# From the output projection to the FFN: the last unit's sums kept apart, second PSUM banks, narrow idle products, wide closing sums, and the first decays one unit later

## The chip, the cores and the metric

The kernel runs on one core of a Trainium2 chip. The metric is the device time of one launch in microseconds (us). Five engines work side by side, each through its own queue in order: TensorE (PE, matrix products), VectorE (DVE), ScalarE (ACT), GpSimd (POOL) and SyncE (SP, which issues most transfers). Engines wait for each other through semaphores. Products land in PSUM, which has eight banks; everything else on the chip lies in SBUF.

## What is computed

One layer of a hybrid diffusion backbone, for 128 context tokens and 256 latent tokens of width 2048 (T = 384 tokens in all):

```python
mod = silu(cond) @ w_ada + b_ada                 # sh1, sc1, ga1, sh2, sc2, ga2
h = rmsnorm(x, norm_pre_mix) * (1 + sc1) + sh1
m, s_f, s_b = mixer(h, ...)                      # gated linear attention and a 2-D DFT branch,
                                                 # merged by sigmoid gates, then @ w_out
x = x + ga1 * rmsnorm(m, norm_post_mix)
h = rmsnorm(x, norm_pre_ffn) * (1 + sc2) + sh2
ff = (silu(h @ w_ffn_gate) * (h @ w_ffn_up)) @ w_ffn_down
x = x + ga2 * rmsnorm(ff, norm_post_ffn)
```

The attention needs a decay per token and channel: `log_sigmoid(lr @ w_a2 + b) / 16`, summed along the tokens of a chunk. The change touches the two lines in the middle (the second norm of the mixer's output and the norm ahead of the FFN), the attention's first decays, and the last norm.

## The kernel before, in words

All activations lie transposed: 128 channels on the partitions, the 384 tokens along the free axis, so a width of 2048 is KT = 16 tiles of 128x384. Weights come in blocks of 128x1024 (512 KB). Each float32 block is split into a high part `whi` (ACT, line 224) and a rest `wlo` (DVE, line 225), and each product is made of three passes: high by high, high by rest, rest by high (`gemm`, line 258). The order of the work on PE, ACT, DVE and POOL is written out by hand in the program; SP's transfers are issued in program order too. Side work runs as Python generators that are advanced by one turn after each half unit of products (`step`): the adaptive modulation of later stages (`ada_rest`, each turn two DVE instructions over 1024 columns, a cycle of 18 turns), and in the gate stage the attention (`gla`).

**Gate stage.** 32 gate units of two halves each advance `gla` and the modulation by a turn. Per head, `gla` makes the decay logits `z` on PE (line 649), turns them into `la` on ACT and DVE (lines 657 to 661), splits `la` into `lah` and `lal`, and in the next turn PE sums them along the tokens (`bT`, line 671), for the forward and then for the backward direction. A head takes 14 turns, and the last norm another three.

**Output projection.** 16 units `m = w_out @ merged`, each followed by `wout`: the tile's square is added to `qs[0]`, the tile times the gate `ga1` goes to `mg32(i)`, its product with `x1(i)` to `qs[1]`, and its square to `qs[2]`. The last unit is followed by `wout_last`: it leaves the square in a tile of its own, forms the other two from the bank with the gate as an operand, ACT and DVE by turns, and adds to `qs[1]`.

**Passage to the FFN.** `wide_sum` sums `qs` over the channels on PE (a product with ones, 64 columns); the results lie in the banks `pst[0]` and `pst[1]`. From the first sum follows the factor `r[:, 0]` (a root on ACT, a reciprocal on DVE); `rows2` spreads it over the partitions (`prow`). From the other two sums and the first factor follows, in four small DVE steps, the mean square of the new `x`, so `r[:, 1]` and the second spread `prow2`. `res_m` and `res_a` form the new x1 tile: DVE multiplies `mg32(k)` by `prow`, and POOL (DVE for tile 0) adds it to `x1(k)`. Then `mg32` of the last tile is made on DVE (line 1147).

**Head of the FFN.** The first three FFN units (HEAD = 3) run side by side over the 16 tiles, nine products a tile (line 1201). `res_b` normalises tile k into `z` (DVE; ACT scales and shifts, lines 1169 and 1173) and gives the high part `h2[0]`; `res_c` gives the rest `h2[1]`. Tiles 0, 9 and 12 (`fused`) take another form: DVE scales, ACT shifts, each in two pieces (128 and 256 tokens) in one bank (lines 1161 and 1165). x1 runs three tiles ahead (LAG = 3): three tiles are made before tile 0 is normalised.

**FFN and end.** The rest of the FFN follows unit by unit. At the end `tok_sum` sums the squares (one column, line 292), `r3` and its spread `prowE` follow, and the tiles of the output are finished on three routes (PE, POOL and DVE) and stored through ACT's and SP's queues.

Of the kernel before, what the change touches and what calls it, by code (L numbers as in the profile page):

```python
# [11 lines left out]
F32 = mybir.dt.float32  # L12
# [84 lines left out]
def tile_step(ctx: ExitStack, tc: tile.TileContext, a, o):  # L97
# [498 lines left out]
    with ExitStack() as s:  # L596
# [23 lines left out]
        def gla():  # L620
# [10 lines left out]
            for h in range(NH):  # L631
# [387 lines left out]
    with ExitStack() as s:  # L1019
# [28 lines left out]
        def wout_last(p, i):  # L1048

            sq0, sq2 = (pe.tile([P, T], F32, tag="sq", name="sq") for _ in range(2))  # L1050
            pr = pe.tile([P, T], F32, tag="sg", name="pr")
            ACT.activation(sq0, p, AF.Square)
# [11 lines left out]
        for i in range(KT):  # L1064
            p = psm.tile([P, T], F32, tag="mm", name="pmm")
            for g in range(2):
# [20 lines left out]
                if g:  # L1087
                    if i < KT - 1:
                        wout(p, i)
                    else:  # L1090
                        sq0, sq2 = wout_last(p, i)
                step(ada)
            if i == KT - 4:
                for _ in ada_gen:
# [1 line left out]

        pst = [pss.tile([P, 2, 3, 64], F32, tag="side", name=f"pst{n}") for n in range(2)]

        def wide_sum(dst, src):
            for t in range(3):
                PE.matmul(dst[:, t, :], src[:, t * P : (t + 1) * P], ones[:, 0:64], start=True, stop=True)

        r = pe.tile([P, 2, 3], F32, name="r12", bufs=1)
        u = pe.tile([P, 2, 3], F32, name="u12", bufs=1)
# [9 lines left out]
        DVE.tensor_copy(u[:, 0, :], pst[0][:, 0, :, 0])  # L1116
# [4 lines left out]
        DVE.tensor_add(qs[2], qs[2], sq2)  # L1121
        wide_sum(pst[1][:, 1], qs[2])
        rows2(prow, 0)
        DVE.scalar_tensor_tensor(u[:, 0, :], pst[1][:, 1, :, 0], 0.5, r[:, 0, :], op0=ALU.mult, op1=ALU.mult)
        DVE.tensor_add(u[:, 0, :], u[:, 0, :], pst[1][:, 0, :, 0])
        DVE.scalar_tensor_tensor(u[:, 1, :], u[:, 0, :], 2.0 / D, r[:, 0, :], op0=ALU.mult, op1=ALU.mult)
        DVE.tensor_add(u[:, 1, :], u[:, 1, :], msx)

        t1s = {}

# [4 lines left out]
        def res_a(k):  # L1135

            (POOL if k else DVE).tensor_add(x1(k), t1s.pop(k), x1(k))

        res_m(0)
        rsqrt(r[:, 1, :], u[:, 1, :], 1.0)  # L1140
        rows2(prow2, 1)
        for k in range(3):
            if k:
                res_m(k)
            res_a(k)
        for lo, hi, c in segs:
            DVE.tensor_scalar_mul(mg32(KT - 1)[:, lo:hi], p[:, lo:hi], mods[:, 2, KT - 1, c : c + 1])

        h2 = alloc_A()
        hp = [  # L1150
            (pss if u == 0 else psm).tile([P, T], F32, tag="mm" if u else "side", name="pmm") for u in range(HEAD)
        ]
        zt = [pss.tile([P, T], F32, tag="side", name="z") for _ in range(2)]
        fused = (0, 9, 12)

        def res_b(k):

            z = zt[k % 2]
            if k in fused:
                for lo, hi, c in segs:  # L1160
                    DVE.scalar_tensor_tensor(
                        z[:, lo:hi], x1(k)[:, lo:hi], mods[:, 4, k, c : c + 1], prow2[:, lo:hi],
                        op0=ALU.mult, op1=ALU.mult,
                    )
                    ACT.activation(h2[0][:, k, lo:hi], z[:, lo:hi], AF.Identity, bias=mods[:, 3, k, c : c + 1])
            else:
                DVE.tensor_mul(z, x1(k), prow2)
                for lo, hi, c in segs:
                    ACT.activation(
                        z[:, lo:hi], z[:, lo:hi], AF.Identity,  # L1170
                        bias=mods[:, 3, k, c : c + 1], scale=mods[:, 4, k, c : c + 1],
                    )
                ACT.copy(h2[0][:, k, :], z)

        def res_c(k):
            z = zt[k % 2]
            if k in fused:
                for lo, hi, c in segs:
                    DVE.scalar_tensor_tensor(
                        h2[1][:, k, lo:hi], z[:, lo:hi], mods[:, 3, k, c : c + 1], h2[0][:, k, lo:hi].bitcast(F32),  # L1180
                        op0=ALU.add, op1=ALU.subtract,
# [2 lines left out]
                DVE.tensor_sub(h2[1][:, k, :], z, h2[0][:, k, :].bitcast(F32))  # L1184


        LAG = 3
# [99 lines left out]
        DVE.tensor_copy(r3, pst[:, 0:3])  # L1287
        DVE.tensor_add(r3, r3, pys[0][:, 0:3])
        rsqrt(r3, r3, 1.0 / D)
        put(pe_ks[0], psm, "mm")  # L1290
        for t in range(3):
# [117 lines left out]
```

## Time and profile before

| | us |
|---|---|
| median of 3 runs | 2034.55 (2034.52 to 2034.64) |
| the profiled execution | 2032.79 |
| its span, first to last instruction | 2031.0 |
| PE busy | 2014.6 (99%) |
| DVE busy | 1251.2 (62%) |
| ACT busy | 770.4 (38%) |
| POOL busy | 34.2 (2%) |

The page of the profile lists busy time per engine over the span. Other views answer for a stretch: the list of waits (engine, line and tile that waited, what ended the wait, total, times, longest), the timeline (start, duration, engine, line, operation, output and inputs, shape, count, and in brackets the idle time before it and what ended it), and stretches (length, busy time of PE, weight loads, DVE, ACT and POOL, then the granted clock of PE as a share of full speed, then transfers). PEld is the loading of weights into PE. A float32 product shows as two passes. Ends of PE instructions are modelled, since products overlap.

### The profile page before, as it was taken

What the parts mean: (1) busy time and instruction counts of PE and PEld (TensorE: products, weight loads), DVE (VectorE), ACT (ScalarE), POOL (GpSimd) and SP (SyncE); (2) the same over time, 40 slices, a digit from 0 to 9 for tenths busy, and PEclk for the clock granted to TensorE, in tenths of its full rate; (3) what the DMA queues carried; (4) which work ended last, traced back from release to release, by engine and by line L of the source; (5) the groups of instructions that cost most, each with busy time, mean ns of one, the idle gap of its engine ahead of it and who ended that gap; (6) DMA issues with size and microseconds to landing.
All of it is one profiled execution on the core that took longest, in us unless ns stands there. A gap on an engine that the chain in (4) does not pass through costs nothing.

```text
span 2031.0 us, 30079 instructions
## 1 busy us (share of the span) xinstructions
PE 2014.6 (99%) x12236; PEld 1959.9 (96%) x12236; DVE 1251.2 (62%) x1655; ACT 770.4 (38%) x1144; POOL 34.2 (2%) x46
## 2 busy tenths in 40 slices
PE   8999999999999999989999999999999999999999
PEld 5779999999999999989999999999999999999998
DVE  5669787898677778866444545453545454544345
ACT  4233545443346544446233222222222222222235
POOL 0000000000000000002000000000000000000001
PEclk9999999999999999999999999999999999999999
DMA  9978677767546785533444444443444444433332
GB/s 390 371 254 276 206 239 233 246 223 261 210 154 207 256 282 185 193 125 115 145 148 147 151 146 147 151 148 125 145 145 146 147 149 150 138 133 125 126 130 97
DMA packets 112395, 373.94 MB, mean 184 GB/s; under 512 B 13692, under 2 KB 32316, under 8 KB 108160
## 3 DMA queue, kind: packets, MB, share of 16 engines
q1 hardware_dynamic: 111248, 370.64, 53.2%
q8 instruction: 96, 1.57, 0.3%
q10 hardware_dynamic: 1008, 1.38, 0.2%
q14 instruction: 43, 0.35, 0.0%
HBM read 358.34 MB, written 13.63 MB: 183 GB/s over the span
## 4 chain that ended last, share of the span: by engine, by line
PE 98%; ACT 1%; DVE 1%; issue 0%; DMA 0%; ACTq 0%; DVEq 0%
PE pmm L258 67%; PE pdn L258 18%; PE pv L399 3%; PE pf L258 2%; PE pgm L382 1%; PE pmm L1201 1%; PE px L417 1%; PE px L300 0%; PE po L629 0%; PE pr L564 0%; PE py L1278 0%; PE pgm L496 0%; PE dl L629 0%; PE pp L856 0%; PE px L870 0%; PE bT L671 0%
## 5 line engine op out<-in xcount | busy, mean ns | idle before, releaser
L258 PE MATMUL pmm<-A_hi,whi 128*128 128x384 f32 x2480 | 831.8, 335 | 0.0
L258 PE MATMUL pmm<-A_hi,wlo 128*128 128x384 f32 x2480 | 828.9, 334 | 0.0
L258 PE MATMUL pmm<-A_lo,whi 128*128 128x384 f32 x2480 | 828.8, 334 | 0.0
L225 DVE TENSOR_TENSOR wlo<-raw,whi 128x1024 fp32r<-128x1024 f32 x434 | 529.8, 1223 | 416.8 <-ACT whi L224 415.6
L224 ACT CAST whi<-raw 128x1024 fp32r<-128x1024 f32 x436 | 457.5, 1050 | 582.4 <-PE pmm L258 226.9
L258 PEld LDWEIGHTS pmm<-A_hi,whi 128*128 128x128 f32 x2480 | 465.6, 188 | 2.9 <-issue 1.8
L258 PEld LDWEIGHTS pmm<-A_lo,whi 128*128 128x128 f32 x2480 | 465.7, 188 | 0.2
L258 PEld LDWEIGHTS pmm<-A_hi,wlo 128*128 128x128 f32 x2480 | 465.6, 188 | 0.0
L556 DVE SCALAR_TENSOR_TENSOR adacc<-adaw,spad,adacc 128x1024 f32<-128x1024 f32 x240 | 296.9, 1278 | 1.2 <-DMA adaw<-in_w_ada 1.0
L258 PE MATMUL pdn<-hid_hi,whi 128*128 128x384 f32 x704 | 235.2, 334 | 0.0
L258 PE MATMUL pdn<-hid_hi,wlo 128*128 128x384 f32 x704 | 235.1, 334 | 0.0
L258 PE MATMUL pdn<-hid_lo,whi 128*128 128x384 f32 x704 | 235.1, 334 | 0.0
L258 PEld LDWEIGHTS pdn<-hid_hi,whi 128*128 128x128 f32 x704 | 132.2, 188 | 0.4 <-issue 0.4
L258 PEld LDWEIGHTS pdn<-hid_lo,whi 128*128 128x128 f32 x704 | 132.2, 188 | 0.0
L258 PEld LDWEIGHTS pdn<-hid_hi,wlo 128*128 128x128 f32 x704 | 132.2, 188 | 0.0
L284 ACT CAST hid_hi<-hfE 128x384 fp32r<-128x384 f32 x44 | 22.6, 513 | 164.0 <-DVE hfE L1224 164.0
L1224 DVE TENSOR_TENSOR hfE<-sg,pmm 128x384 f32<-128x384 f32 x44 | 24.4, 555 | 84.6 <-PE pmm L258 84.0
L1216 ACT ACTIVATE sg<-pmm 128x384 f32<-128x384 f32 x44 | 21.6, 492 | 136.3 <-PE pmm L258 136.2
L1241 DVE TENSOR_TENSOR Blo<-Blo,pdn 128x384 f32<-128x384 f32 x72 | 39.5, 553 | 47.9 <-PE pdn L258 47.9
L1241 DVE TENSOR_TENSOR Bhi<-Bhi,pdn 128x384 f32<-128x384 f32 x72 | 39.1, 549 | 34.1 <-PE pdn L258 34.0
L258 PE MATMUL pmm<-o_hi,whi 128*128 128x384 f32 x128 | 42.8, 335 | 0.0
L258 PE MATMUL pmm<-o_lo,whi 128*128 128x384 f32 x128 | 42.8, 334 | 0.0
(309 smaller groups left out, 1520.9 us busy)
## 6 DMA issues: line engine op xcount, KB each, us to landing
adaw<-in_w_ada SPq DMA_DIRECT2D x128, 512.0 KB, 3.9
raw<-in_w_g SPq DMA_DIRECT2D x88, 512.0 KB, 3.2
raw<-in_w_u SPq DMA_DIRECT2D x88, 512.0 KB, 3.3
raw<-in_w_d SPq DMA_DIRECT2D x88, 512.0 KB, 3.2
slab<-in_w_ada SPq DMA_DIRECT2D x32, 1024.0 KB
raw<-in_w_gate SPq DMA_DIRECT2D x64, 512.0 KB, 4.5
raw<-in_w_in SPq DMA_DIRECT2D x44, 512.0 KB, 3.2
raw<-in_w_out SPq DMA_DIRECT2D x32, 512.0 KB, 4.5
```

Of the source, the lines that this page charges most:

```text
L224: ACT.copy(hi, raw)
L225: sub = lambda: eng.tensor_sub(lo, raw, hi.bitcast(F32))
L258: PE.matmul(dst, w[wi][:, k * n + n0 : k * n + n0 + P], x[xi][:, k0 + k, :], start=first and k == 0 and j == 0, stop=last and k == kts - 1 ...
L284: ACT.copy(hi, src)
L382: PE.matmul(pgv[q : q + 32, :], spad[:, k, :], slab[k // (KT // 2)][:, k % (KT // 2), :], start=k < 4, stop=k >= KT - 4,)
L399: PE.matmul(pv[2 * t + g], hT[x_][:, kb, t * P : (t + 1) * P], w_[:, g * 512 : (g + 1) * 512], start=kb == 0 and j == 0, stop=kb == KT - 1 ...
L417: PE.matmul(px, w_[:, u * P : (u + 1) * P], hT[x_][:, kb, :], start=j == 0, stop=j == 2)
L556: DVE.scalar_tensor_tensor(acc[:, c, :], w, spad[:, k, c : c + 1], acc[:, c, :], op0=ALU.mult, op1=ALU.add,)
L1201: PE.matmul(hp[u], hw[u][j][:, ((k - 1) % 8) * P : ((k - 1) % 8 + 1) * P], h2[m][:, k - 1, :], start=k == 1 and j == m == 0, stop=k == KT ...
L1216: ACT.activation(sgs[j], p, AF.Silu)
L1224: DVE.tensor_mul(hf, sgs.pop(j), p)
L1241: DVE.tensor_add(acc(k), acc(k), p)
```

## The change

It has five edits.

1. In the attention, head 0 gives up two turns between the decays' split and the first `bT` products; all that follows in `gla` comes two turns later.
2. `wout_last` now makes `mg32` of the last tile on ACT, as in the other units, and returns three tiles (the square, room for the product with x1, and the square of `mg32`). ACT reads the bank alone. The three sums have banks of their own (`E0`, `S0`) or share one that is read when both are there (`S12`). The addition to `qs[1]` and `qs[2]` is done ahead of one sum each, and the sum of the last square is added between them. The scaling of line 1147 is gone.
3. The banks of the head units are taken earlier, and PE makes narrow products of ones by ones (128 columns) into one of them: two after `prow`, four after `prow2`. The head's first product starts that bank anew.
4. Two x1 tiles instead of three are made before tile 0 is normalised; the third follows right behind it. The second piece of a fused tile has a bank of its own (`zx`).
5. At the end `wide_sum` (64 columns) takes the place of `tok_sum`.

```diff
                 split_act(lah, lal, la)
                 yield
+                if h == 0:
+                    yield
+                    yield
                 for d in range(2):
...
             ACT.activation(sq0, p, AF.Square)
             for lo, hi, c in segs:
-                g = mods[:, 2, i, c : c + 1]
-                DVE.scalar_tensor_tensor(pr[:, lo:hi], p[:, lo:hi], g, x1(i)[:, lo:hi], op0=ALU.mult, op1=ALU.mult)
-                ACT.activation(sq2[:, lo:hi], p[:, lo:hi], AF.Square, scale=g)
-            DVE.tensor_add(qs[1], qs[1], pr)
-            return sq0, sq2
+                ACT.mul(mg32(i)[:, lo:hi], p[:, lo:hi], mods[:, 2, i, c : c + 1])
+            ACT.activation(sq2, mg32(i), AF.Square)
+            return sq0, pr, sq2
...
-        wide_sum(pst[0][:, 0], qs[0])
-        DVE.tensor_copy(u[:, 0, :], pst[0][:, 0, :, 0])
-        wide_sum(pst[0][:, 1], sq0)
-        DVE.tensor_add(u[:, 0, :], u[:, 0, :], pst[0][:, 1, :, 0])
+        wide_sum(E0[:, 0], qs[0])
+        wide_sum(S0[:, 0], last3[0])
+        DVE.tensor_copy(u[:, 0, :], E0[:, 0, :, 0])
+        DVE.tensor_mul(last3[1], mg32(KT - 1), x1(KT - 1))
+        for n in (1, 2):
+            DVE.tensor_add(qs[n], qs[n], last3[n])
+            wide_sum(S12[:, n - 1], qs[n])
+            if n == 1:
+                DVE.tensor_add(u[:, 0, :], u[:, 0, :], S0[:, 0, :, 0])
         rsqrt(r[:, 0, :], u[:, 0, :], 1.0 / D)
-        wide_sum(pst[1][:, 0], qs[1])
-        DVE.tensor_add(qs[2], qs[2], sq2)
-        wide_sum(pst[1][:, 1], qs[2])
         rows2(prow, 0)
...
+        def narrow_warm(n):
+            for _ in range(n):
+                PE.matmul(hp[1][:, 0:P], ones, ones, start=True, stop=True)
+
+        narrow_warm(2)
         res_m(0)
-        rsqrt(r[:, 1, :], u[:, 1, :], 1.0)
+        rsqrt(r[:, 1, :], u[:, 0, :], 1.0)
         rows2(prow2, 1)
-        for k in range(3):
+        narrow_warm(4)
+        LAG = 3
+        for k in range(LAG - 1):
             if k:
                 res_m(k)
             res_a(k)
-        for lo, hi, c in segs:
-            DVE.tensor_scalar_mul(mg32(KT - 1)[:, lo:hi], p[:, lo:hi], mods[:, 2, KT - 1, c : c + 1])
...
+        zx = psm.tile([P, T], F32, tag="mm", name="zx")
+        def z_of(k, lo):
+            return zx if lo else zt[k % 2]
...
         for k in range(KT + 1):
             if k < KT:
                 res_b(k)
+            if k == 0:
+                res_m(LAG - 1)
+                res_a(LAG - 1)
             if k:
                 res_c(k - 1)
...
-        tok_sum(pst[:, 0:3], qs[0], *late)
-        tok_sum(pys[0][:, 0:3], last_sq)
+        pst, ps2 = (t.rearrange("p (t c) -> p t c", t=3)[:, :, 0:64] for t in (pst, pys[0]))
+        wide_sum(pst, qs[0], *late)
+        wide_sum(ps2, last_sq)
```

More of the change, by code (lines that the diff above doesn't have):

```diff
@@ L1090, in tile_step @@
                     else:
-                        sq0, sq2 = wout_last(p, i)
+                        last3 = wout_last(p, i)
                 step(ada)
@@ L1095, in tile_step, with wide_sum @@
                     pass
-        pst = [pss.tile([P, 2, 3, 64], F32, tag="side", name=f"pst{n}") for n in range(2)]
-        def wide_sum(dst, src):
+        E0, S0, S12 = (pss.tile([P, 2, 3, 64], F32, tag="side", name="pst") for _ in range(3))
+        def wide_sum(dst, *src):
             for t in range(3):
-                PE.matmul(dst[:, t, :], src[:, t * P : (t + 1) * P], ones[:, 0:64], start=True, stop=True)
+                for n, x in enumerate(src):
+                    PE.matmul(
+                        dst[:, t, :], x[:, t * P : (t + 1) * P], ones[:, 0:64], start=n == 0, stop=n == len(src) - 1,
+                    )
         r = pe.tile([P, 2, 3], F32, name="r12", bufs=1)
@@ L1137, in res_a @@
             (POOL if k else DVE).tensor_add(x1(k), t1s.pop(k), x1(k))
+        hp = [
+            (pss if u == 0 else psm).tile([P, T], F32, tag="mm" if u else "side", name="pmm") for u in range(HEAD)
+        ]
+        def narrow_warm(n):
+            for _ in range(n):
+                PE.matmul(hp[1][:, 0:P], ones, ones, start=True, stop=True)
+        narrow_warm(2)
         res_m(0)
-        rsqrt(r[:, 1, :], u[:, 1, :], 1.0)
+        rsqrt(r[:, 1, :], u[:, 0, :], 1.0)
         rows2(prow2, 1)
-        for k in range(3):
+        narrow_warm(4)
+        LAG = 3
+        for k in range(LAG - 1):
             if k:
@@ L1160, in res_b @@
                 for lo, hi, c in segs:
+                    z = z_of(k, lo)
                     DVE.scalar_tensor_tensor(
@@ L1178, in res_c @@
                 for lo, hi, c in segs:
+                    z = z_of(k, lo)
                     DVE.scalar_tensor_tensor(
@@ L1283, in tile_step @@
         last_sq = late.pop()
-        tok_sum(pst[:, 0:3], qs[0], *late)
-        tok_sum(pys[0][:, 0:3], last_sq)
+        pst, ps2 = (t.rearrange("p (t c) -> p t c", t=3)[:, :, 0:64] for t in (pst, pys[0]))
+        wide_sum(pst, qs[0], *late)
+        wide_sum(ps2, last_sq)
         r3 = pe.tile([P, 3], F32, name="r3", bufs=1)
-        DVE.tensor_copy(r3, pst[:, 0:3])
-        DVE.tensor_add(r3, r3, pys[0][:, 0:3])
+        DVE.tensor_copy(r3, pst[:, :, 0])
+        DVE.tensor_add(r3, r3, ps2[:, :, 0])
         rsqrt(r3, r3, 1.0 / D)
```

12 lines of the change are left out of this document (4 added, 8 removed).

## The prediction

> **What bounds the kernel now.** I read the page's busy shares first, then the list of waits of TensorE (PE), then the timeline around the longest of them, then the granted clock in short stretches there.
>
> ```profile
> span 2031.0 us, 30079 instructions
> PE 2014.6 (99%) x12236; PEld 1959.9 (96%) x12236; DVE 1251.2 (62%) x1655; ACT 770.4 (38%) x1144; POOL 34.2 (2%) x46
> PE pmm L1201 <- ACT A_hi L1165: 2.1, 1, 2.1
> PE pst L1103 <- DVE u L1116: 2.0, 1, 2.0
> ...
> PE prow L1111 <- DVE r L304: 0.8, 1, 0.8
> PE bT L671 <- DVE lal L285: 0.7, 1, 0.7
> PE pst L1103 <- DVE qs L1121: 0.6, 1, 0.6
> ```
>
> PE is busy for 99% of the span, so time is to be had only where it waits or runs slowly. Four of the waits shown (2.1, 2.0, 0.8 and 0.6, together 5.5 us) lie in one place, the passage from the output projection to the FFN; a fifth, 0.7, stands before the first decay products. In the passage (start, duration):
>
> ```profile
> 898.25 0.78 PE L1103 MATMUL pst<-ones,qs 128*128 128x64 f32 x6
> 898.45 0.49 ACT L1052 ACTIVATE sq<-pmm 128x384 f32<-128x384 f32 x1 [3.28 <-PE pmm L258]
> ...
> 901.06 0.85 PE L1103 MATMUL pst<-ones,sq 128*128 128x64 f32 x6 [2.03 <-DVE u L1116]
> ...
> 903.14 0.88 PE L1103 MATMUL pst<-ones,qs 128*128 128x64 f32 x6 [0.56 <-DVE qs L1121]
> ...
> 903.86 1.44 PE L1111 MATMUL prow<-ident,r 128*128 128x128 f32 x6
> ...
> 904.64 0.16 DVE L1127 TENSOR_TENSOR u<-u,msx 128x3 f32<-128x3 f32 x1
> ...
> 905.34 0.55 DVE L1133 TENSOR_TENSOR t<-Bhi,prow 128x384 f32<-128x384 f32 x1 [0.53 <-PE prow L1111]
> 905.81 0.17 DVE L304 RECIPROCAL r<-r 128x3 f32<-128x3 f32 x1
> ...
> 906.12 1.62 PE L1111 MATMUL prow<-ident,r 128*128 128x128 f32 x6 [0.82 <-DVE r L304]
> ...
> 907.33 0.74 DVE L1147 TENSOR_SCALAR Blo<-pmm,mods 128x128 f32<-128x128 f32 x2
> 907.98 0.34 DVE L1161 SCALAR_TENSOR_TENSOR z<-Chi,mods,prow 128x128 f32<-128x128 f32 x1
> ...
> 908.76 0.49 DVE L1161 SCALAR_TENSOR_TENSOR z<-Chi,mods,prow 128x256 f32<-128x256 f32 x1 [0.43 <-ACT A_hi L1165]
> ...
> 909.29 0.47 ACT L1165 ACTIVATE A_hi<-z,mods 128x256 fp32r<-128x256 f32 x1 [0.56 <-DVE z L1161]
> ...
> 909.81 1.33 PE L1201 MATMUL pmm<-A_hi,whi 128*128 128x384 f32 x3 [2.07 <-ACT A_hi L1165]
> ```
>
> This is a serial chain: sums over channels on PE, small VectorE (DVE) steps, a root, a broadcast (prow), a second root, a second broadcast, and the first normalised tile. Granted clock (first number after the busy times) in stretches:
>
> ```profile
> 903.50:904.00 0.50, 0.50 (x6) 0.50 (x6) 0.00 (x0) 0.00 (x0) 0.00 (x0) 1.00 0.00 0
> 904.00:904.50 0.50, 0.50 (x5) 0.50 (x4) 0.37 (x3) 0.00 (x0) 0.00 (x0) 0.52 0.00 0
> ...
> 914.20:914.40 0.20, 0.20 (x3) 0.20 (x2) 0.20 (x2) 0.17 (x2) 0.00 (x0) 0.85 0.00 0
> ...
> 2016.50:2017.00 0.50, 0.50 (x6) 0.50 (x5) 0.00 (x0) 0.00 (x0) 0.00 (x0) 0.76 0.00 0
> 2020.00:2020.50 0.50, 0.50 (x2) 0.19 (x1) 0.50 (x2) 0.00 (x0) 0.50 (x1) 0.82 0.00 0
> ```
>
> A mean of 0.52 over 904.00 to 904.50 puts the drop to half clock at 904.02; 0.85 over 914.20 to 914.40 puts the return at 914.26. So both broadcasts and the first two tiles run at half clock, for 10.24 us. The tail has the same from 2016.76 (0.76) to 2020.18 (0.82), 3.42 us.
>
> **The change, part by part.** Edits that cost nothing: sums in banks of their own and the reordered names move no work; the two wider sums at the end issue as many passes as before.
>
> *Decays.* The two empty turns give ScalarE and DVE one unit more for the chain that ended 0.7 late. The branch takes 59 turns now, so 61 of the 64 half-units that the 32 gate units offer; nothing is left to run uncovered. Heads 1 to 3, the state loads and stores on SP, and the memsets on POOL move by the same two turns with their order among themselves kept; only head 0 is in the list of waits, although the heads already meet the modulation work at different places of its 18-turn cycle. Bounds 0 and 0.7; I take 0.7, from the row that exists.
>
> *Chain up to the first FFN product.* Prices of the steps that take the place of others: two ScalarE products by the gate, and DVE's elementwise 0.55 above.
>
> ```profile
> 2012.31 0.79 ACT L1255 ACTIVATE Blo<-ff,mods 128x128 f32<-128x128 f32 x2
> ```
>
> The square ends at 898.94 as now; the two gate products end at 899.73; DVE's product and its two additions (0.55 each) end at 900.28, 900.83 and 901.38. The sum of the squares, in its own bank, has been done meanwhile (it waited 2.03 for a DVE read of the shared bank). The two remaining sums on PE run 900.83 to 902.53 at 0.85 each; today the last ends at 903.14 + 0.88 = 904.02. That is 1.49 earlier. What follows keeps its distances: the small DVE steps end 904.80 - 904.02 = 0.78 after the sums, and prow, the first x1 product, the reciprocal and prow2 stay in their order, so prow2 ends at 907.74 - 1.49 = 906.25 at half-clock prices. The first z then starts at 906.29, since the two products of L1147 (0.74) that pushed it to 907.98 are gone from its queue; the second half, no longer waiting 0.43 for ScalarE to leave the bank, follows 0.35 later, ends at 907.13, ScalarE ends 0.04 + 0.47 later, and the first FFN product starts at 907.69, 2.12 earlier. If the clock holds, each broadcast goes from 1.44 and 1.62 to about the 1.09 that the tail's six passes took:
>
> ```profile
> 2016.13 1.09 PE L1292 MATMUL prowE<-ident,r 128*128 128x128 f32 x6
> ```
>
> That is 0.35 + 0.53 more, so a start at 906.81, 3.0 earlier.
>
> *Idle products.* Two (four passes) lie between prow and prow2, four (eight passes) behind prow2. At 1.09/6 = 0.18 a pass the eight take 1.45, which fits ahead of 906.81; at half clock, 1.62/6 = 0.27 or, by 1.44/6, 0.24, they end near 908.0, so they would hold the first product by some 0.3. Covered by PE's own waiting, they cost nothing at full clock.
>
> *The head of the FFN.* Sixteen tiles, nine products each, fed by DVE and ScalarE:
>
> ```profile
> 911.31 0.48 ACT L1173 CAST A_hi<-z 128x384 fp32r<-128x384 f32 x1
> ...
> 912.83 0.48 ACT L1173 CAST A_hi<-z 128x384 fp32r<-128x384 f32 x1
> ...
> 915.08 0.68 PE L1201 MATMUL pmm<-A_hi,whi 128*128 128x384 f32 x3
> ...
> 928.14 0.49 DVE L1161 SCALAR_TENSOR_TENSOR z<-Clo,mods,prow 128x256 f32<-128x256 f32 x1 [0.56 <-ACT A_hi L1165]
> ...
> 931.10 0.48 ACT L1173 CAST A_hi<-z 128x384 fp32r<-128x384 f32 x1
> ...
> 932.24 0.68 PE L1201 MATMUL pmm<-A_hi,whi 128*128 128x384 f32 x3
> ...
> 936.91 0.33 PE L258 MATMUL pmm<-A_hi,whi 128*128 128x384 f32 x1
> ```
>
> The casts shown are of tiles 1, 2 and 13. Tile 2 is ready at 913.31, but PE, slow on tiles 0 and 1, takes it at 915.08; from there 14 tiles need 21.83, 1.559 each. The feed bounds the gain. The third x1 tile now stands between z of tile 0 and z of tile 1 (about +0.5 on DVE), against the 0.43 saved; so tiles 1 and 2 come as much earlier as z of tile 0: 1.69 at half clock, 2.57 at full. I take 2.5, so tile 2 at 910.8 and PE on it at once, 4.2 to 4.3 earlier than 915.08; that hides a short wait for tiles 0 and 1. Late next is tile 13, with a slack of 932.24 - 931.58 = 0.66: its feed gains 2.5 and the waits for the bank in tiles 9 and 12 (the row shows 0.56), some 3.5, which with 0.66 covers 4.2 just. POOL still adds x1 three tiles ahead. Bounds: 5.2, if sixteen tiles of 1.559 follow 906.81 without a wait; 1.2, if the clock is at half until a window edge in tile 2. I take 4.2.
>
> *Tail.* The sums gain nothing themselves (64 columns instead of one, six passes at 0.85 above against 0.83 in the row below), but they give PE more to do before the drop at 2016.76, and everything arrives some 5 us earlier against the clock's edges.
>
> ```profile
> 2014.51 0.83 PE L292 MATMUL pys<-ones,sq 128*128 128x1 f32 x6
> ...
> 2024.75 0.54 DVE L1313 TENSOR_TENSOR yE<-Blo,prowE 128x384 f32<-128x384 f32 x1
> ...
> 2025.88 1.45 PE L1314 MATMUL py<-yE,ident 128*128 128x384 f32 x4
> ...
> 2028.13 0.34 ACTq L1303 DMA_DIRECT2D out_yT<-Clo  x1
> ```
>
> At full clock PE saves half of 3.42, 1.7; then its last product waits for DVE's factor (2025.29) instead of ending at 2027.33, and ends near 2026.1. So at most 1.3 to 1.6; none if the drop stays, and 0.05 lost with the sums. I take 1.2.
>
> **The sum.** 0.7 + 4.2 + 1.2 = 6.1. The profiled execution took 2032.79, 1.79 more than its span; the change stays inside the span, so that execution would take 2026.7. The median of the runs is 2034.55, 1.76 above it, and I carry the difference over: 2028.4.
>
> The drop and return are 10.24 apart. The Trainium skill, page "TensorE: Matmul & The Clock Gate", part 1, says that activity is judged in free-running windows of 3.413 us; 10.24 is three of them, so the trace agrees. By it the verdict depends on where an edge falls, which is the second case below.
>
> **Rivals.**
> *The clock drops in the passage anyway.* The stretch of 3.4 us before 904.02 held eighteen narrow passes and one of prow; after the change a stretch from about 898.9 to 902.3 holds much the same, the idle products coming later. For it: that stretch. Against it: the longest gap of PE shrinks from 2.0 to about 1.1, and the idle products fill the later ones, so that half clock should last one window. Then the passage gives 2.5 (tiles 0 and 1 partly slow, 0.3 for the idle products) to 3.5, with 0.7 and 0.6 in the tail: 2034.55 - 4.5 = 2030.0.
>
> *The change does not do what it says.* The head becomes bound by its feed, and an earlier start is handed back: if tiles came every 1.7 instead of 1.559, 14 of them lose 2.0, and with the decays' wait merely moved and no gain in the tail 4.2 - 2.0 = 2.2 is left: 2032.4. For it: feed and PE are within some 0.02 us a tile of each other. Against it: casts 1 and 2 are 1.52 apart, below 1.559.
>
> *Slower.* The same place, further: the late x1 addition of tile 2 on POOL reaches z of tile 2 late, and the ring of three x1 tiles passes the delay on to each. It decides from 6.1/14 = 0.44 a tile on, tiles every 2.0 us; at 2.2 us 14 tiles lose 9.0: 2037.4. Against it: DVE runs the same instructions per tile, and its 0.56 of waiting is removed.
>
> **Chances.** Forecast 58% (own range 2027.0 to 2029.8), clock drop 22%, given back 12%, slower 8%. The range reaches from the bounds 0.7 + 5.2 + 1.6 = 7.5, 2027.0, to 2031.6, in the gap between the clock's case and the third. A fifth of a per cent, 4.1 us, is about what a measurement can tell, so faster begins at 2030.48: all but 2 of the 58, 14 of the 22 and 2 of the 12 make 72%; slower 8%; the rest 20%.
>
> **What would show it.** Right: no wait before the decay products; the first FFN product about 8.7 us after the last product of the projection (now 11.4), tile 2 within 13 (now 16.7), granted clock 1.0 through the passage and through the tail's broadcasts. Wrong: half clock in tiles 0 to 2; waits of PE on A_hi or A_lo beyond tile 1; new waits in the gate units of heads 1 to 3, whose decays now fall on other modulation steps; a last store still bound by DVE.

## The result, and the profile after

| | before | after |
|---|---|---|
| median of 8 runs each, side by side on one chip | 2034.56 us (2032.77 to 2036.81) | 2028.93 us (2026.65 to 2030.84) |
| ratio, with its 95% interval | | 0.9971 (0.9961 to 0.9980) |
| the profiled execution | 2032.79 | 2029.43 |
| its span | 2030.97 | 2027.65 |

The change makes the kernel 5.6 us faster (0.29%); 2028.4 was forecast. The two profiled executions differ by only 3.4: before's lies 1.77 below its median, after's 0.50 above. Cut at four marks (the first decay logits, the last product of the output projection, the first product of the fourth FFN unit, the last product of the FFN), the spans compare so:

| stage, us | before | after | forecast for the difference | found |
|---|---|---|---|---|
| start, to the first decay logits | 204.97 | 206.53 | 0 | +1.56 |
| to the last product of the projection | 693.11 | 692.22 | -0.7 | -0.89 |
| passage and head of the FFN | 38.83 | 35.28 | -4.2 | -3.55 |
| rest of the FFN | 1076.03 | 1076.02 | 0 | -0.01 |
| tail, to the end of the span | 18.03 | 17.60 | -1.2 | -0.43 |

The start is code that no edit touches. Its +1.56 goes with a spell of half clock that this execution happened to have: over the thirteen profiles of this document a start with such a spell takes 206.4 to 206.7, one without 204.9 to 205.7. Without the start the stages sum to -4.9. In the stretches below (length, busy time of PE, weight loads, DVE, ACT, POOL, granted clock, transfers), from the start of the kernel after, the clock goes to 0.50 at 21.80 and comes back at 25.21 (0.90 over 21 to 22 and over 25 to 26):

```profile
21.00:22.00 1.00, 0.80 (x3) 0.71 (x4) 0.82 (x2) 0.14 (x1) 0.00 (x0) 0.90 1.04 434
22.00:24.00 2.00, 2.00 (x6) 1.62 (x6) 1.34 (x2) 0.00 (x0) 0.00 (x0) 0.50 0.98 386
25.00:26.00 1.00, 1.00 (x24) 0.58 (x20) 0.21 (x1) 0.00 (x0) 0.00 (x0) 0.90 1.03 418
```

The list of PE's waits of the kernel after, where before had 2.1, 2.0, 0.8, 0.7 and 0.6:

```profile
PE pst L1105 <- DVE qs L1124: 0.9, 1, 0.9
...
PE pmm L1222 <- ACT A_hi L1183: 0.5, 1, 0.5
...
PE pmm L1222 <- DVE A_lo L1198: 0.2, 1, 0.2
PE pmm L1222 <- ACT A_hi L1191: 0.2, 1, 0.2
```

The decays' wait (`bT`) is gone from the list, and 1.8 us are left in the passage. The same place in the timeline of after:

```profile
898.75 0.33 PE L258 MATMUL pmm<-A_hi,wlo 128*128 128x384 f32 x1
898.93 0.78 PE L1105 MATMUL pst<-ones,qs 128*128 128x64 f32 x6
...
899.67 0.88 PE L1105 MATMUL pst<-ones,sq 128*128 128x64 f32 x6
...
901.48 1.98 PE L1105 MATMUL pst<-ones,qs 128*128 128x64 f32 x12 [0.93 <-DVE qs L1124]
...
903.25 1.59 PE L1115 MATMUL prow<-ident,r 128*128 128x128 f32 x6
...
905.66 0.99 PE L1115 MATMUL prow<-ident,r 128*128 128x128 f32 x6
...
908.01 0.79 PE L1222 MATMUL pmm<-A_hi,whi 128*128 128x384 f32 x3 [0.45 <-ACT A_hi L1183]
...
934.03 0.33 PE L258 MATMUL pmm<-A_hi,whi 128*128 128x384 f32 x1
```

The reader is to see that the two sums that waited 2.0 and 0.6 now wait once, 0.93; that the first broadcast still takes 1.59 while the second takes 0.99; and that the first product of the FFN comes 908.01 - 898.75 = 9.26 after the last product of the projection (11.73 before). The granted clock in three stretches of 3.41 us there (length, busy time of PE alone, granted clock, transfers):

```profile
899.02:902.43 3.41, 2.48 (x22) 1.00 0.32 124
902.43:905.85 3.42, 3.42 (x17) 0.50 0.00 0
905.85:909.26 3.41, 2.96 (x20) 1.00 0.02 5
```

Half clock for 3.42 us, from 902.43, where before had 10.24. So it is the forecast's second case that this execution shows: the clock drops all the same, for one window.

### The profile page after: what moved, and what is told of

Read it like the earlier page. It is cut to its first block, busy times and chain, and to the rows that moved or that the text cites. A ratio compares the mean times of both kernels' runs of the same rounds, so it can differ in the third digit from the quotient of the medians.

```text
span 2027.7 us, 30109 instructions
## 1 busy us (share of the span) xinstructions
PE 2014.5 (99%) x12248; PEld 1959.0 (97%) x12248; DVE 1250.4 (62%) x1652; ACT 770.2 (38%) x1145; POOL 34.2 (2%) x46
## 4 chain that ended last, share of the span: by engine, by line
PE 98%; DVE 1%; DMA 0%; ACT 0%; issue 0%; SPq 0%; ACTq 0%; DVEq 0%
PE pmm L258 67%; PE pdn L258 18%; PE pv L399 3%; PE pf L258 2%; PE pgm L382 1%; PE pmm L1222 1%; PE px L417 1%; PE po L629 0%; DMA Clo<-in_xT 0%; PE pr L564 0%; PE dl L629 0%; PE pgm L496 0%; PE pp L859 0%; PE px L873 0%; PE bT L674 0%; PE at L714 0%
```

## The experiments

Two theories of where the forecast's terms went were to be told apart. The first: the passage is a serial chain, and how long it lasts depends, beside the chain, on where the clock drops, so that after and its variants move by whole windows of the clock. The rival: the head of the FFN is bound by its feed (DVE, ScalarE, GpSimd), so that an earlier start is handed back over the 16 tiles. "Passage" is the length from the last product of the projection to the first product of the fourth FFN unit, "tail" that from the last product of the FFN to the end of the span; both are of the run's profile, which is one execution. Medians stand beside a median of before of 2034.5 to 2034.8 on the same chip. The three groups of runs below come from three chips, so between groups the ratios compare better than the medians.

| kernel | median (range, runs) | ratio, 95% interval | passage | tail |
|---|---|---|---|---|
| before + edit 1 | 2034.30 (2033.23 to 2035.98, 10) | 0.9996 (0.9987 to 1.0006) | 39.82 | 18.59 |
| after without idle products | 2030.96 (2027.12 to 2031.92, 8) | 0.9975 (0.9965 to 0.9986) | 36.80 | 17.63 |
| after + four more idle products | 2028.75 (2027.07 to 2029.13, 5) | 0.9967 (0.9954 to 0.9980) | 34.10 | 17.62 |
| after with narrow closing sums | 2029.36 (2028.11 to 2031.85, 9) | 0.9972 (0.9962 to 0.9982) | 35.29 | 17.56 |

**Edit 1 alone.** On the kernel before:

```diff
                 split_act(lah, lal, la)
                 yield
+                if h == 0:
+                    yield
+                    yield
```

> The kernel before with the decays' two empty turns alone. Theory: the wait of 0.7 us in front of bT goes and no new wait comes in the gate units, so the stretch from the first z product of head 0 to the last product of the output projection, 693.1 us before, becomes 692.2 to 692.5, as in the changed kernel (692.2); the passage to the FFN stays near 38.8 and the tail near 18.1. Rival (the wait only moves): a wait of the same size appears at bT or at a later head and the stretch stays at 693.1. In time both are close: 2033.8 against 2034.6, inside the spread of the runs.

The `bT` wait is gone, and the stretch from the first decay logits to the last product of the projection goes from 693.11 to 692.23, which is 0.88 (0.89 in the full change). No new wait of PE takes its place. The median cannot show it: 0.88 us is 0.04%, and this execution had the clock at half in the passage for 13.65 us, four windows instead of three, and so a passage of 39.82. Its tail of 18.59 is taken up below.

**No idle products.** The kernel after without its six:

```diff
-        narrow_warm(2)
         res_m(0)
...
-        narrow_warm(4)
```

> The changed kernel without the six narrow idle products (they add nothing to the result). Clock theory: once the clock has dropped in the passage it stays at half for two or three stretches of 3.41 us instead of one, so both broadcasts and some of tile 0 and 1 are slow again; the passage (last product of the projection to the first product of the fourth FFN unit) is 36.0 to 37.2 instead of 35.3, the time 0.7 to 1.9 us above the changed kernel. Feed theory: the head waits for DVE and ScalarE in any case, so the passage stays at 35.1 to 35.5 and the idle products are worth nothing.

The first product of the FFN still starts 9.26 after the last of the projection: the drop comes later in the chain, so the first broadcast is shorter (1.35 against 1.59) and the second longer (1.62 against 0.99). But the clock, which dropped at 903.30, stays at half until 913.54:

```profile
904.00:906.00 2.00, 1.18 (x6) 0.91 (x6) 1.58 (x4) 0.30 (x1) 0.00 (x0) 0.50 0.00 0
906.00:908.00 2.00, 0.83 (x4) 0.54 (x3) 1.16 (x5) 0.71 (x2) 1.01 (x1) 0.50 0.05 8
...
912.00:914.00 2.00, 2.00 (x9) 2.00 (x8) 1.91 (x5) 1.89 (x5) 1.50 (x2) 0.62 0.00 0
```

That is 10.24 us, three windows, against one in after. It costs 36.80 - 35.28 = 1.52 in the passage; the medians are 2.0 apart, but the intervals of the two ratios overlap. So the six idle products do not keep the clock from dropping; in this pair of executions it comes back after one window with them and after three without.

It is one pair, in which the drop does not lie at the same place of the chain, and the long spell does not come every time. Each run's mean granted clock is on record, 0.001 of it is about 4 us at half clock, and three of these eight runs (2027.12 to 2029.05) have 0.999, where the profiled one has 0.997. Beside before, which also had 10.24 us at half clock and a passage of 38.83, the 36.80 shows about what the shorter chain and the second banks are worth with the clock at half for as long: 2.03.

**Four more idle products, where PE still waits 0.93.** On the kernel after:

```diff
+        for _ in range(4):
+            PE.matmul(S12[:, 1, 0:2, :], ones, ones, start=True, stop=True)
         DVE.tensor_copy(u[:, 0, :], E0[:, 0, :, 0])
         DVE.tensor_mul(last3[1], mg32(KT - 1), x1(KT - 1))
```

> The changed kernel with four more idle products (eight passes) between the sum of the last square and the two sums after it, where PE waits 0.93 us; they go to a bank that the next sums overwrite. Clock theory: the stretch that now holds only narrow sums is filled, the clock does not drop in the passage, the two sums and both broadcasts take their full-clock durations (1.7, about 1.0 and 1.0 in place of 1.98, 1.59 and 0.99), the first tile comes 0.7 to 1.0 us earlier and the passage is 34.2 to 34.7. Feed theory: the broadcasts are faster, but the head starves for as much, and the passage stays at 35.1 to 35.5.

The timeline of this kernel:

```profile
897.52 0.33 PE L258 MATMUL pmm<-A_hi,wlo 128*128 128x384 f32 x1
...
899.15 1.11 PE L1122 MATMUL pst<-ones 128*128 128x128 f32 x8
900.25 1.55 PE L1105 MATMUL pst<-ones,qs 128*128 128x64 f32 x12
901.64 0.89 PE L1115 MATMUL prow<-ident,r 128*128 128x128 f32 x6
...
905.60 0.80 PE L1224 MATMUL pmm<-A_hi,whi 128*128 128x384 f32 x3 [0.46 <-ACT A_hi L1185]
```

The granted clock is 1.00 throughout the passage. The twelve passes of the sums take 1.55 instead of 1.98, the broadcast 0.89 instead of 1.59, and the FFN starts 8.08 after the projection. Passage 34.10, a little below the 34.2 to 34.7 expected and 4.73 below before, between the 4.2 forecast for a full clock and its bound of 5.2. Tile 1 comes 2.50 after tile 0 and tile 2 another 1.67; from there the tiles follow at 1.56 to the end. So the feed holds the first two tiles by about 1.05 in all, and no more of the start is handed back. The medians of after and of this kernel (2028.93, 2028.75) do not differ; what differs is the passage of the two profiles. The full clock is no accident of one execution: in all seven profiles with these four products (this one and six below) it is full in the passage, in the three without them (after, without idle products, narrow closing sums) it drops there.

**Narrow sums at the end.** On the kernel after:

```diff
-        wide_sum(pst, qs[0], *late)
-        wide_sum(ps2, last_sq)
+        tok_sum(pst[:, 0:3], qs[0], *late)
+        tok_sum(pys[0][:, 0:3], last_sq)
...
-        DVE.tensor_copy(r3, pst[:, :, 0])
-        DVE.tensor_add(r3, r3, ps2[:, :, 0])
+        DVE.tensor_copy(r3, pst[:, 0:3])
+        DVE.tensor_add(r3, r3, pys[0][:, 0:3])
```

> The changed kernel with the closing sums of one column again. The prediction gave the tail 1.2 us and the changed kernel's tail (last FFN product to the end of the span) is only 0.4 shorter, 17.65 against 18.06, although the clock stayed full in it. If the wide sums hold the clock in the tail, the clock drops again here by the time of the broadcast or the first output products, and the last store on ScalarE's queue goes from 13.8 us after the last FFN product back to about 15.2, with the end of the span 0.2 to 0.5 later. If the clock there is a matter of where its edges fall, or the tail is bound by GpSimd's and SP's route, the tail is within 0.2 of 17.65 whatever the clock does.

Tail 17.56 against 17.60, and the clock is full in both while PE works. Edit 5 is worth nothing here. That the tail now runs at full clock has another reason, and its place among the clock's windows is the likely one: counted in steps of 3.413 from the drops seen, a window starts 0.41 after the FFN's last product in before, and the clock drops at its end; in after one starts 1.71 behind that product, here 1.58. What the wide sums would do at before's place no run shows. The kernel before with idle products (below) has before's closing sums, a full clock and a tail of 17.57.

The next four were run together; the first three stand on the kernel with four more idle products, the fourth on the kernel before.

| kernel | median (range, runs) | ratio, 95% interval | first FFN product | passage |
|---|---|---|---|---|
| + three x1 tiles ahead of tile 0 | 2028.04 (2027.72 to 2028.29, 5) | 0.9968 (0.9956 to 0.9980) | 8.33 | 33.93 |
| + without the bank `zx` | 2029.77 (2028.52 to 2030.06, 9) | 0.9975 (0.9966 to 0.9985) | 8.61 | 35.69 |
| + idle products in the start | 2027.92 (2027.41 to 2029.16, 6) | 0.9968 (0.9956 to 0.9979) | 8.08 | 34.11 |
| before + idle products alone | 2033.65 (2031.17 to 2034.23, 10) | 0.9995 (0.9986 to 1.0004) | 11.73 | 38.34 |

**Three x1 tiles first, as before.**

```diff
-        for k in range(LAG - 1):
+        for k in range(LAG):
...
-            if k == 0:
-                res_m(LAG - 1)
-                res_a(LAG - 1)
```

> The changed kernel with the filled gap (e3_fill, passage 34.10 at full clock throughout), and three x1 tiles made before tile 0 is normalised, as before the change. Feed theory: DVE is idle for some 0.2 us before the second broadcast ends, so the third product delays z of tile 0 by only 0.2 to 0.3, and z of tile 1 then comes 0.2 to 0.3 earlier than with the product between them; PE waits less at tile 0's second part and at tile 1, and the passage is 33.8 to 34.1. As the reordering would have it: tile 0 comes 0.4 to 0.5 later and nothing is won back, passage 34.5 to 34.6.

Tile 0 starts 0.25 later, tile 1 at 10.36 instead of 10.58, and the passage is 0.17 shorter. So the new place of the third x1 tile, which the forecast had cost at nothing (0.5 lost against 0.43 saved), gives back a little; the last kernel below, which has it too, repeats the passage (33.91).

**One bank for both pieces.**

```diff
-            return zx if lo else zt[k % 2]
+            return zt[k % 2]
...
-        zx = psm.tile([P, T], F32, tag="mm", name="zx")
```

> The changed kernel with the filled gap, and both pieces of tiles 0, 9 and 12 in one bank again. If the wait for the bank counts: the second piece of tile 0 waits 0.4 for ScalarE, the first product comes 0.4 later, and with the waits of 0.5 in tiles 9 and 12 the feed falls behind PE by tile 13 (its slack was 0.66 before the change and PE is 4.7 us earlier now): passage 34.5 to 35.2, with waits of PE on A_hi after tile 9. If only tile 0 counts: 34.5 without later waits. If the wait is hidden: 34.1.

The passage grows by 35.69 - 34.10 = 1.59, more than foreseen. DVE's second piece waits again for ScalarE to leave the bank, in tiles 0, 9 and 12; the last two in the timeline:

```profile
920.89 0.49 DVE L1180 SCALAR_TENSOR_TENSOR z<-Clo,mods,prow 128x256 f32<-128x256 f32 x1 [0.51 <-ACT A_hi L1184]
...
926.20 0.49 DVE L1180 SCALAR_TENSOR_TENSOR z<-Clo,mods,prow 128x256 f32<-128x256 f32 x1 [0.56 <-ACT A_hi L1184]
```

0.53 of the 1.59 come at tile 0 (8.61 against 8.08), the rest from tile 9 on: tile 10 starts 1.85 after tile 9, and 1.56 with `zx`. With the start this early, the feed would bind without the second bank. With it, it does not.

**Idle products in the start too.**

```diff
             prev = new
+            if kb == 0:
+                for _ in range(7):
+                    PE.matmul(pv[5][:, 0:P], ones, ones, start=True, stop=True)
         qk =
```

> The changed kernel with the filled gap and seven more idle products (fourteen passes) in the first stage, where PE waits 1.7 us for the first normalised tile; they go to a bank that is first written later. Clock theory: the half-clock stretch at 22 to 25 us, which the changed kernel's profile has and that of the kernel before has not, does not occur, the first z product of the attention comes at 205.0 to 205.4 in the profile, and the runs lie within 2 us of each other (they spread over 4.2 for the changed kernel), with a median 0.3 to 1.0 below that of e3_fill. Rival: the spread comes from elsewhere, and stays at 3 to 4 us.

No half clock in the passage, the tail or the stretch from 20 to 30 us of this execution, and its runs lie within 1.75 us where those of after spread over 4.2. The first decay logits come at 205.71, not at the 205.0 to 205.4 that were expected. Five of the six runs have a mean granted clock of 1.000, the slowest (2029.16) among them, which leaves no room for a whole window at half, so the spread that is left is not the clock's. Of the nine profiles without these products six have a spell of half clock between 21 and 26 us, of the four with them none. In the median 2027.92 and after's 2028.93 cannot be told apart, the intervals of the ratio overlapping.

**Idle products on the kernel before**, eight, two and eight, with nothing else changed:

```diff
         wide_sum(pst[0][:, 0], qs[0])
+        idle(8)
...
         rows2(prow, 0)
+        idle(2)
...
         rows2(prow2, 1)
+        idle(8)
```

> The kernel before with idle products alone: eight behind the first sum, two behind the first broadcast, eight behind the second, its chain of sums and tiles as it was. Clock theory: no half clock in the passage, both broadcasts 0.35 and 0.5 to 0.6 shorter, first head product at 10.7 to 11.0 after the last projection product instead of 11.7, tile 2 as soon as its feed allows, passage 36.0 to 36.6 instead of 38.8. So of the 4.7 us between 38.8 and 34.1 the clock alone would give 2.2 to 2.8 and the shorter chain the rest. Rival: without the shorter chain the clock gives only the broadcasts, passage 37.5 to 38.

The passage is 38.34, neither the 36 to 36.6 that were expected nor the rival's 37.5 to 38, and the first FFN product comes no earlier. The clock is at half for one window, 906.42 to 909.84, not three, yet only 0.49 comes of it: tile 9 starts 26.39 after the projection, and from there on the tiles come 1.85, 1.67, 1.79 and 1.85 apart instead of 1.56, behind waits for the shared bank. That is the slack of 0.66 at tile 13 that the prediction counted. So the idle products without the second bank pay 0.49 here, with one window still at half; the second bank without the idle products was not run. The worth of the two together does not follow from a run of one alone.

The last three take up the tail, whose term had failed. Their base is the kernel with idle products in start and passage (tail 17.58).

**The first store earlier.** VectorE's first product with the factor is put ahead of ScalarE's copy of it:

```diff
-        ACT.copy(rr, prow)
...
             DVE.tensor_mul(y, acc(k), prow)
+            if n == 0:
+                ACT.copy(rr, prow)
...
+        on_pe(0)
         for k in pool_ks:
             on_pool(k)
-        for n in range(2):
-            on_pe(n)
+        on_pe(1)
```

> The variant with the start and the passage filled with idle products, and in the tail VectorE's first product with the factor is put ahead of ScalarE's copy of the factor (and of GpSimd's first tile, which needs that copy). If the tail is bound by the transfers of the output from the first store on, what counts is when the first store starts: VectorE gets the factor 0.5 earlier, the first store starts about 6.3 us after the last product of the FFN (6.8 so far), and the tail falls from 17.6 to 17.1, although GpSimd's tiles come 0.5 later. If the tail is bound by the work on the tiles, the later GpSimd leaves it at 17.6 or takes it to 18.1. Time 2027.4 by the first, 2027.9 to 2028.4 by the second.

2027.32 (2026.67 to 2028.96, 5 runs), ratio 0.9966 (0.9953 to 0.9978), tail 17.59. The first store starts 6.66 after the last product of the FFN, not 6.3: VectorE is earlier, but TensorE takes up its product only behind two others already in its queue. And the transfer engines are not kept full behind it (share 0.88 in the stretch from 2017.50 to 2018.00). With 0.14 gained at the first store this tells the two readings of the tail apart no better than before.

**Four of sixteen output tiles not stored.**

```diff
-            if n in (1, 2, 3, 4):
-                store(pool_ks.pop(0), SP)
             store(k, SP)
```

> The same variant without the move in the tail, and the four output tiles that GpSimd makes are computed but not stored, so 12 of 16 tiles reach the output. Bound by transfers: 0.79 MB less at 367 GB/s is 2.1 us less to move, so the tail falls from 17.6 until the last store of ScalarE's queue (13.8) and its own landing of 2.0 to 2.8 set the end: 15.8 to 16.6. Bound by the work on the tiles: nothing changes, 17.6.

2026.13 in its only run. Tail 16.79, so 0.79 less: the transfers did set the end. But they do so by 0.8 only, and not by the 2.1 that they take themselves. The stretches of this kernel (last two numbers: share of the transfer engines, GB/s):

```profile
2018.00:2020.00 2.00, 1.95 (x7) 0.93 (x6) 2.00 (x5) 0.66 (x2) 1.92 (x3) 1.00 0.71 256
...
2022.00:2023.00 1.00, 0.00 (x0) 0.00 (x0) 0.00 (x0) 0.00 (x0) 0.00 (x0) 1.00 0.74 267
```

The engines now have gaps, and what ends last is the last store of ScalarE's queue: issued at 13.76 after the last product of the FFN, moved by about 15.2 (0.74 of the stretch from 2022.00, if they lie at its front), with some 1.6 from there to the end of the span. The expected 15.8 to 16.6 had left that last part out.

**All that has paid, together**: the idle products, three x1 tiles first and the earlier first store.

> All that has paid together: idle products in the start and ahead of the pair of sums, three x1 tiles ahead of tile 0, and VectorE's first product ahead of ScalarE's copy in the tail. If the gains add up: passage 33.9, tail 17.1, clock full everywhere, 0.2 + 0.5 below the variant with the fills: 2027.2. If the last two give nothing, 2027.9.

2027.22 (2026.81 to 2029.05, 5 runs), ratio 0.9966 (0.9952 to 0.9979); passage 33.91, tail 17.60, clock full. It is the lowest median, 1.7 below after, but the intervals overlap; the passage is what was expected, the tail is not. This profile and that of the earlier first store lose 1.3 to 1.5 between the first decay logits and the end of the projection (693.51 and 693.74 against 692.22), 0.5 to 0.8 of it in waits for VectorE ahead of the products of the branch, in code that none of these edits touches. The kernel before with idle products has it too (693.89 against 693.11). It looks like a matter of the single execution: these profiled executions took 2028.46 and 2028.96, and their kernels have runs of 2026.81 and 2026.67. What brings it about was not tried.

## Why the prediction was right, and which term was not

Of the signs that were named, the wait before the decays went, the list shows no wait on A_hi or A_lo beyond tile 1, and the clock held in the tail's broadcast. The clock of 1.0 through the passage did not come in after's profile; it came with four more idle products. The first FFN product, "about 8.7" behind the end of the projection's last (the sum itself gave 8.4 and, at half clock, 9.28), is 8.93 behind it in after and 7.75 with the full clock.

**Decays** (0.7 forecast, 0.88 and 0.89 found). The bound taken from the one row that existed was right: the wait went, and the later heads met no new one.

**The chain up to the first FFN product.** Its order came as laid out. After's timeline lies 0.68 behind the prediction's (first sum at 898.93, there at 898.25), so 0.68 is added to each forecast time. The late sums were to start at 900.83 + 0.68 = 901.51 and start at 901.48. With half clock the first FFN product was forecast at 907.69 + 0.68 = 908.37 and is at 908.01; with full clock at 906.81 + 0.68 = 907.49, and the run with a full clock has it 8.08 after the start of the projection's last product, which is 906.83 on this scale. Tile 2, forecast within 13 of that product's end, is 13.1 behind it in after (13.42 - 0.33) and 11.9 with the full clock. The 0.66 between is mostly in the prices of the narrow passes: six passes of a broadcast take 0.89 and 0.91 at full clock, not 1.09 (0.38 for two), and twelve passes of sums 1.55, not 1.70 (0.15).

**Idle products** were to hold the first product by 0.3 at half clock; nothing of it shows. Their worth lay elsewhere: in the profile without them the half clock lasts 10.24 us and not 3.41.

**The head of the FFN.** The 4.2 forecast is the passage with a full clock; 4.73 was found there (34.10), and 3.55 in after's own profile, where one window is at half: the upper end of the second case's 2.5 to 3.5. How often a run of after gets the one or the other is told only by its mean granted clock: two of the eight runs have 1.000 (2026.65 and 2028.11), so no whole window at half anywhere; four have 0.997 or 0.998 (2029.24 to 2030.84), so 6 us or more of it, in the passage or elsewhere. The third case and the slower one fall: the tiles come at 1.56, and only without `zx` did they come at more. That the two waits of 0.56 in tiles 9 and 12 were needed as cover, with the slack of 0.66, is what the runs without `zx` and with the idle products alone show. The third x1 tile's move was priced at zero and costs 0.17.

**The tail** (1.2 forecast, at most 1.3 to 1.6; 0.4 found). This is the step that failed. The clock is at full through the sums, the broadcast and the products of the tiles, as forecast, and the work on the tiles does end 1.4 earlier: the last store of ScalarE's queue was 2028.13 - 2012.94 = 15.19 after the FFN's last product and is now 2023.82 - 2010.05 = 13.77 after it. The first and the last store of that queue in the timeline of after:

```profile
2016.85 0.37 ACTq L1325 DMA_DIRECT2D out_yT<-Chi  x1
...
2023.82 0.34 ACTq L1325 DMA_DIRECT2D out_yT<-Clo  x1
```

But the term had no price for the transfers. Stretches of the kernel before (last two numbers: share of the transfer engines, GB/s):

```profile
2020.20:2022.00 1.80, 1.80 (x6) 0.87 (x5) 1.80 (x5) 0.82 (x2) 1.72 (x3) 1.00 0.53 189
2022.00:2024.00 2.00, 2.00 (x8) 1.19 (x7) 2.00 (x6) 0.62 (x2) 1.92 (x3) 1.00 1.00 362
...
2026.00:2028.00 2.00, 1.33 (x5) 0.45 (x3) 0.00 (x0) 0.86 (x2) 0.06 (x1) 1.00 1.02 368
...
2029.50:2030.00 0.50, 0.00 (x0) 0.00 (x0) 0.00 (x0) 0.00 (x0) 0.00 (x0) 1.00 0.35 126
```

And of the kernel after:

```profile
2016.90:2019.00 2.10, 2.10 (x8) 1.31 (x8) 2.10 (x6) 0.96 (x2) 2.02 (x4) 1.00 0.61 217
2019.00:2021.00 2.00, 2.00 (x8) 1.21 (x7) 2.00 (x6) 0.48 (x1) 1.92 (x4) 1.00 1.02 366
...
2023.00:2025.00 2.00, 0.27 (x1) 0.00 (x0) 0.00 (x0) 0.48 (x1) 0.08 (x1) 1.00 1.02 367
...
2026.00:2026.50 0.50, 0.00 (x0) 0.00 (x0) 0.00 (x0) 0.00 (x0) 0.00 (x0) 0.50 0.73 249
```

In both kernels the transfer engines are full (1.00 to 1.02, 362 to 368 GB/s) from about 0.9 us after the issue of the first store (a share of 0.61 over the 2.10 us from 2016.90 in after is 1.28 us of full engines, from 2017.72 on) to some 1.3 us before the end of the span. 16 tiles of 192 KB are 3.15 MB, 8.6 us at 367 GB/s. So the end follows the first store by 0.9 + 8.6 + 1.3 = 10.8. In before that store goes out on SP's queue:

```profile
2020.21 2.23 SPq L1303 DMA_DIRECT2D out_yT<-Chi  x4
```

That is 2020.21 - 2012.94 = 7.27 after the FFN's last product; now it is 2016.85 - 2010.05 = 6.80, 0.47 earlier, and the tail is 0.43 shorter. The other profiles agree: in the ten that store all tiles in this order the first store lies 6.74 to 7.83 after the FFN's last product, and the end follows it by 10.76 to 10.83 every time. The longest tail, 18.59 with edit 1 alone, has its first store at 7.83; there too the clock was at half in the tail, from 2016.18 to 2019.59. In the two with the first store pulled ahead the end follows by 10.93 and 10.94; the engines of the first of them have the gap named above. The run with twelve stores confirms it from the other side: with less to move, the tail falls to 16.79, where the work on the tiles ends it, 3.03 after the issue of its last store. By the same 3.03, which is an estimate for another kernel, the work of before would have ended at 15.19 + 3.03 = 18.2, about where its tail ended (18.03): the two ends lay close together there, and taking 1.4 off the one left the other. The sign that was named for a failure here, "a last store still bound by DVE", is not what came; the stores are bound by one another. The Trainium skill, page "DMA: Bandwidth & Descriptors", section Specifications, gives about 358 GB/s as the share of one core in the memory's bandwidth; the stores here, at 362 to 368, agree with it within 3%, while the loads in the start, 434 GB/s in the first row of the stretches from the start, go beyond it.

**The sum.** 6.1 forecast, 5.6 in the medians. In the profiles it is 0.89 + 3.55 + 0.43 = 4.9 with one window at half clock in the passage, and 0.88 + 4.73 + 0.41 = 6.0 in the run that has none. Where the clock holds, the sum comes out near because a passage that is 0.5 better than its forecast and decays that are 0.2 better make up for a tail that is 0.8 worse. In after's own profile nothing makes up for it: 2026.7 was forecast for the profiled execution and it took 2029.43, with 1.56 of the difference in the start. That the median is within 0.5 all the same is in part luck. The forecast let the profiled execution lie as far below the median after the change as before it (1.76); it lay 0.50 above.

## What to carry to other kernels

A stage that ends in stores has two ends, that of the work and that of the transfers: divide the bytes by the rate that the stretches show (here 3.15 MB by 367 GB/s) from the first store on, before a gain in the work is put into the sum. In a serial chain of small steps, fill what TensorE waits with idle narrow products, and look where the clock's drop lies in more than one execution before a difference of a few us is read as one of the kernel. Two changes that each open the same stage (an earlier start, a faster feed) are not to be measured one at a time and added.

## What the hardware showed beside that

The clock's spells of half speed were 3.41, 10.24 and 13.65 us long in all these profiles (the last one of each, after PE's work, is cut off by the end): one, three and four times 3.41. What lies between two spells is whole windows too: from 914.258 to 2016.763 in before it is 1102.5 us, 323.0 times 3.4133. The Trainium skill, page "TensorE: Matmul & The Clock Gate", part 1, gives a free-running window of 3.413 us, which agrees. What decides a window does not: the page has the clock fall after a window of idling, and its closing rules speak of idle gaps above some 3 us; here PE's longest wait ahead of the drop is 0.93 (after), and the measurement decides. Nor does the busy share that the profile shows settle it. The stretches of before, each one window long:

```profile
897.19:900.60 3.41, 1.84 (x14) 1.70 (x12) 1.15 (x3) 1.18 (x3) 0.00 (x0) 1.00 0.71 226
900.60:904.02 3.42, 2.40 (x19) 2.29 (x20) 1.09 (x5) 0.45 (x2) 0.00 (x0) 1.00 0.00 0
...
2013.35:2016.76 3.41, 3.37 (x24) 2.67 (x24) 1.57 (x5) 1.10 (x3) 0.00 (x0) 1.00 0.01 2
```

After the first, with PE busy for 1.84 of 3.41, the clock stays; after the second, with 2.40, it drops; after the third, in the tail, it drops with 3.37. What the gate counts, if these are its windows, is left open. It is one thing that makes the time of one and the same kernel vary: after's runs at a mean clock of 1.000 took 2026.65 and 2028.11, the one at 0.997 took 2030.84. Before and after each spread over 4.0 to 4.2 us in eight runs, where the three runs shown ahead of the prediction had agreed within 0.12.
